# A new opening, and output and last down projections taken one token tile after the other, in a two-layer hybrid decoder trunk

## The chip, the cores and the metric

The kernel runs on one core of a Trainium2 chip. Five engines with queues of their own matter here: PE (matrix products and transposes), DVE (vector operations), ACT (scalar operations, which also copies and squares), POOL (small scalar work) and SP (issues transfers). The metric is the device time of one execution in microseconds. Times of single instructions come from one profiled execution.

## The reference

Two decoder layers run over 256 tokens of width 1024, all in float32. What is computed, cut to what matters:

```python
def hybrid_layer(x, ...):
    h = rms_norm(x, attn_pre_gain)
    u = h @ w_in                       # q, k, v of two mixers, gates: 4120 columns
    o_a = swa_sink_attention(...)      # sliding window, with sinks
    o_b = nsa_attention(...)           # compressed + selected + window branches
    mixed = sigmoid(g_a) * (o_a @ w_branch_a) + sigmoid(g_b) * (o_b @ w_branch_b)
    x = x + rms_norm(mixed @ w_out, attn_post_gain)
    h = rms_norm(x, ffn_pre_gain)
    x = x + rms_norm(conv_ffn(h, ffn_w_up, ffn_conv_w, ffn_conv_b, ffn_w_down), ffn_post_gain)
    return x

def rms_norm(x, gain):
    return x * rsqrt(mean(x * x) + EPS) * gain
```

## The kernel before, in words

The 256 tokens are two tiles, t=0 and t=1, of 128. A float32 product is done as three faster products: each operand is split into a rounded high part and the rest, the low part, and `mm3` adds high x high, high x low and low x high. Every weight therefore passes through three steps: a transfer into one of four raw buffers (`st`), a copy on ACT that makes the high part (L114), and a subtraction on DVE that makes the low part (L117). `Stream` keeps the weights in their order of use; `make` does the two splitting steps, and `W.load` the transfer. Most weights go to rings of four high and four low buffers (`wh`, `wl`); a tag in the stream sends a few elsewhere: `kB` (one buffer), `sg` (two buffers, which also hold the gates SG during attention), `q8`. A buffer of a ring can be written again once the last reader of what it held is done.

A layer runs in this order: nine input tiles (`in_tile`, chunks c=0 to 3 of the weights for both token tiles), attention units placed by a table of ticks among them, the two branch products, the output projection (`out_layer`, eight chunks k of `w_out`, for both token tiles, into PSUM banks O for t=0 and S for t=1), the norm after it, the norm before the feed-forward part, and `ffn_layer` (22 column pairs j up, convolution, gate, down).

The order in the source gives only a priority. A scheduler writes the order of each engine's instructions ahead of time, from its own idea of when operands and buffers are there; each engine then executes its list strictly in order. Only the first input tile (L866) is written out by hand for PE, DVE and ACT: there the list follows the source.

At the seam between attention and feed-forward each token tile passes a chain (`after`, L943): two squares of the product on ACT (L362), the reciprocal root on POOL (L354, L355), the residual on DVE (L397), two squares of the new x, the root again, the scaling of x by gain and root (L950, L957), eight transposes on PE (L373), high copy on ACT and low subtraction on DVE (L114, L117). Only then can the first up products (`up_first`) of that tile start.

At the beginning `start` runs zero products to warm TensorE (`warm`), transposes x (`first_T`, L410), scales it by the gain (L412) and splits it (`first_split`); `hooks` places the further pieces between the products of the first tile. `rest` computes the squares of x and the rotary tables, which end on POOL (L348, L349); the rotation of the queries (L466) waits for those.

Of the kernel before, what the change touches and what calls it, by code (L numbers as in the profile page):

```python
# [50 lines left out]
MANUAL0 = {mybir.EngineType.PE, mybir.EngineType.DVE, mybir.EngineType.Activation}  # L51
PLAN = {'A': (23, 24, 24, 34), 'B0': (39, 43), 'B1': (49, 53, 58, 64), 'C': 66, 'S': (56, 75)}
DL = {'qa0': 2, 'qa1': 13, 'ka': 6, 'qb0': 8, 'qr0': 8, 'qb1': 2, 'qr1': 4, 'cb0': 1, 'cb1': 3, 'ks': 1, 'kw': 6, 'pT': (3, 3, 2), 'pv': 4, 'hT': 1, 'ge': 3, 'pj': 4, 'cT': 5, 'cv': 9, 'yT': 1, 'h0': 5, 'h1': 4, 'uf': 0, 'x0': 3, 'x1': 3}
WARM = (6, 8)
HOOKS = {0: '1C', 1: 'B2', 2: 'D', 6: '3r'}
FIRST = [(0, 0), (0, 1), (1, 0), (1, 1), (0, 2), (1, 2), (0, 3), (1, 3)]
CMPI = (0, 0, 0, 0, 4, 6, 7, 8)
AH = (2, 2, 2, 3, 2, 2, 2, 2, 2)
TG = True
# [6 lines left out]
def tile_hybrid_trunk(  # L66
# [78 lines left out]
    class Stream:  # L145
        def __init__(self):
            self.specs, self.loaded, self.made, self.used, self.front = [], {}, {}, 0, 0

        def add(self, src, a, b, tag="w", ahead=2):
            self.specs.append((src, a, b, tag, ahead))  # L150
# [1 line left out]

        def load(self, i):
            src, a, b, tag, _ = self.specs[i]
            st = wp.tile([P, a, b], F32, tag="st", bufs=4, name=nm("st"))
            nc.sync.dma_start(st, src)
            self.loaded[i] = st, a, b, tag

        def make(self, i=None):
            i = self.front if i is None else i  # L160
# [3 lines left out]
        def high(self, i):  # L164
            if i not in self.loaded:
                self.load(i)
            st, a, b, tag = self.loaded.pop(i)
            both = None
            if tag == "w":
                hi = wp.tile([P, a, b], F32R, tag="wh", name=nm("wh"))  # L170
                lo = wp.tile([P, a, b], F32R, tag="wl", name=nm("wl"))
            elif tag in ("q8", "kB"):
                both = ap_.tile([P, 2, a, b], F32R, tag=tag, bufs=TAGS[tag], name=nm(tag))
                hi, lo = both[:, 0], both[:, 1]
            elif tag == "joint":
# [12 lines left out]
            return low
# [11 lines left out]
    def stream_layer(l):  # L200
        off = 0
        jn = 0

        def joint(at_):
            nonlocal jn
            while jn < 8 and CMPI[jn] <= at_:
                W.add(cmp_w1[l, jn].rearrange("p (i h) -> p i h", i=4), 4, P, "joint")
                jn += 1

        for i, (c0, w) in enumerate(IN_TILES):  # L210
            for c in range(4):
                if i == 6:
                    joint(2 * c)
                W.add(w_in[l, off:off + 2 * P * w].rearrange("(p k n) -> p k n", p=P, k=2), 2, w,
                      ahead=0 if i == 1 and c < 2 or i == 0 and l == 0 else AH[i])
                off += 2 * P * w
            if i == 6:
                joint(8)
        for wb in (w_branch_a, w_branch_b):
            v = wb[l].rearrange("(k p) n -> p k n", p=P)  # L220
            for n in range(2):
                for c in range(2):
                    W.add(v[:, 2 * c:2 * c + 2, n * 512:(n + 1) * 512], 2, 512)
        wo = w_out[l].rearrange("(k p) n -> p k n", p=P)
        for k in range(8):
            W.add(wo[:, k:k + 1, :], 1, D, {2: "kB", 5: "sg"}.get(k, "w"), ahead=1 if k > 5 else 2)
        wd = ffn_w_down[l].rearrange("(j p) n -> p j n", p=P)
        wu = ffn_w_up[l]
        for c in range(4):
            W.add(wu[c].rearrange("p (k n) -> p k n", k=2), 2, 512, "q8" if c == 0 else "w", ahead=0)  # L230
        for j in range(2, NJ):
            for half in range(2):
                W.add(wu[2 * j + half].rearrange("p (k n) -> p k n", k=8), 8, P, ahead=0 if j < 3 else 2)
            if LAG <= j < NJ - 2:
                W.add(wd[:, j - LAG:j - LAG + 1, :], 1, D)
        for j in range(NJ - 4, NJ):
            early[l, j] = W.add(wd[:, j:j + 1, :], 1, D, {NJ - 1: "sg", NJ - 2: "kB"}.get(j, "w"))
# [19 lines left out]
    pool.memset(rows, 0.0)  # L257
    grow = k1()[0:KD, 0:P]
    nc.sync.dma_start(cst[:, 0:P], consts[:, 0:P])
    act.dma_start(halves(X[:, 0, :])[0], halves(xv[:, 0, :])[0])  # L260
    nc.sync.dma_start(grow, attn_pre_gain[0].rearrange("(k p) -> k p", p=P))
    W.load(0)
    nc.sync.dma_start(halves(X[:, 0, :])[1], halves(xv[:, 0, :])[1])
    W.load(1)
    nc.sync.dma_start(X[:, 1, :], xv[:, 1, :])
    W.load(2)
    W.load(3)
    last_sq = [None]

    def table(fn):  # L270
# [150 lines left out]
    def attn_layer(l, xp, rs, gains, first):  # L421
# [2 lines left out]
        SG = [ap_.tile([P, QKV], F32, tag="sg", bufs=2, name=nm("SG")) for _ in range(2)]  # L424
        done = set()

        def in_tile(i, tag, fin, tmajor=False, hooks={}):
            c0, w = IN_TILES[i]
            bk = [bank(tag) for _ in range(2)]
# [2 lines left out]
            def go(t, c):  # L432
                if c not in chs:
                    chs[c] = W.next(2, w)
                ch = chs[c]
                tk = slice(t * P, (t + 1) * P)
                for k in range(2):
                    kk = 2 * c + k
                    o, wh, wl = bk[t][:, :w], ch[0][:, k, :], ch[1][:, k, :]
                    if i == 2:  # L440

                        o = o.rearrange("p (y x d) -> p y x d", x=2, y=2)
                        wh, wl = [v.rearrange("p (x y d) -> p y x d", x=2, y=2) for v in (wh, wl)]
                    mm3(o, xh[:, kk, tk], xl[:, kk, tk], wh, wl, kk == 0, kk == 7)
                if c == 3:
                    fin(t, bk[t])
                if tmajor and t == 1 and c < 2:
                    W.make()
# [477 lines left out]
    def out_layer(l, yp, gains):  # L926
# [16 lines left out]
        def after(t):  # L943
            gf = gains["ffn_pre"]
            post_norm(t, res[t], gains["attn_post"])
            xg = k4()
            s2 = mean_sq(halves(X[:, t, :]))
            for n in range(2):
                c = slice(n * 512, (n + 1) * 512)
                dve.tensor_tensor(xg[:, c], X[:, t, c], gf[:, c], ALU.mult)  # L950
            if TG and t == 1:
                with tc.issue_after(last_sq[0].ins):
                    table(AF.Gelu_apprx_tanh)
            r = rstd_of(s2)
            for n in range(2):
                c = slice(n * 512, (n + 1) * 512)
                dve.tensor_scalar(xg[:, c], xg[:, c], r, None, ALU.mult)  # L957
            later(DL["h0"] if t == 0 else DL["h1"], lambda: t8(xg, hp, t))

        order = [(0, k) for k in range(6)] + [(1, 0), (1, 1), (0, 6), (1, 2), (0, 7), (1, 3), (1, 4), (1, 5), (1, 6), (1, 7)]  # L960
        for t, k in order:
            part(lambda: go(t, k))
            if (t, k) in ((0, 7), (1, 4), (1, 5), (1, 7)):
                W.make()
        return hp


    def ffn_layer(l, hp, gains, last):
# [94 lines left out]
        for j in range(2, NJ):  # L1063
# [6 lines left out]
            if j < NJ - 2:  # L1070
                for t in range(2):
                    part(lambda: down(j - LAG, t))
        order = [(NJ - 4, 0), (NJ - 3, 0), (NJ - 2, 0), (NJ - 4, 1), (NJ - 1, 0), (NJ - 3, 1), (NJ - 2, 1), (NJ - 1, 1)]
        rs = [None, None]
        order_ = [None]
        xp = None if last else (big8("x8", 2), big8("x8", 2))
# [40 lines left out]
    def start():  # L1117
# [9 lines left out]
        gb = bank("T")  # L1127
        pe.transpose(gb[:, 0:KD], grow, ident[0:KD, 0:KD])
        dve.tensor_copy(gfirst, gb[:, 0:KD])
        low = first_split(0, 0, first_T(0, 0), xp)  # L1130
        warm(WARM[1])
        lw = W.high(0)
        low()
        lw()

        def xs(*args):
            lows = [first_split(t, h, first_T(t, h), xp) for t, h in args]
            for f in lows:
                f()

        def rest():
            for t in range(2):
                rs[t] = rstd_of(mean_sq(halves(X[:, t, :])))
            dve.tensor_scalar(nsink, sink, -1.0, None, ALU.mult)
            rope_tables()
        act_ = {"B": lambda: xs((0, 1)), "C": lambda: xs((1, 0)), "D": lambda: xs((1, 1)), "X": lambda: xs((1, 0), (1, 1)),
                "1": lambda: W.make(1), "2": lambda: W.make(2), "3": lambda: W.make(3), "r": rest, "w": lambda: warm(3)}
        return {FIRST[i]: [act_[c] for c in h] for i, h in HOOKS.items()}

    more_rows()  # L1150
    later(20, lambda: load_vec(0, 4))
# [84 lines left out]
```

## Time and profile before

| | |
|---|---|
| median of three runs | 794.11 us (791.46 to 797.75) |
| profiled execution, its own time | 794.85 us |
| its span, first to last instruction | 793.0 us |
| PE busy | 765.7 us, 97% of the span |
| DVE busy / ACT busy | 613.2 us / 495.4 us |
| mean granted TensorE clock | 0.992 of full |

The span is a little shorter than the time, since it leaves out what lies before the first and after the last instruction. A busy PE is not PE at its peak: its clock has two levels, and the granted clock of a stretch says which it is.

### The profile page before, as it was taken

How to read it: one execution, taken by the hardware profiler on the slowest of the kernel's cores; microseconds unless marked ns; L12 is line 12 of the kernel's file. 1: busy time of each engine (PE TensorE's matmuls, PEld its weight loads, DVE VectorE, ACT ScalarE, POOL GpSimd, SP SyncE). 2: the span in 40 equal slices, each digit the busy share in tenths (PEclk: the TensorE clock that was granted, in tenths of full speed). 3: DMA queues.
4: the chain of work that ended last, by engine and by line, in shares of the span. 5: the costliest groups of instructions: out<-in, count | busy, mean ns of one | idle time of the engine just before them, and what ended most of it. 6: DMA issues, size and time to landing. Idle time of an engine off the chain costs nothing.

```text
span 793.0 us, 12908 instructions
## 1 busy us (share of the span) xinstructions
PE 765.7 (97%) x4745; PEld 682.0 (86%) x4745; DVE 613.2 (77%) x1168; ACT 495.4 (62%) x948; POOL 48.1 (6%) x96
## 2 busy tenths in 40 slices
PE   8999999999899999999989999999998999999996
PEld 6689888888699999999868889888877999999995
DVE  5898888676778767777788888886867877778775
ACT  4678877744666555665555879767555655556552
POOL 2300022100100000000010000230001000000000
PEclk9999999999999999999999999999999999999999
DMA  7633156456556656666435232644645666656731
GB/s 268 218 111 123 41 160 216 144 172 205 166 168 196 187 185 183 209 218 186 157 118 173 74 121 86 206 151 135 205 137 182 193 185 186 186 184 212 216 105 53
DMA packets 42202, 131.26 MB, mean 166 GB/s; under 512 B 5359, under 2 KB 5915, under 8 KB 42139
## 3 DMA queue, kind: packets, MB, share of 16 engines
q1 hardware_dynamic: 41995, 130.18, 51.4%
q8 instruction: 37, 0.61, 0.3%
q10 hardware_dynamic: 144, 0.26, 0.1%
q14 instruction: 26, 0.21, 0.1%
HBM read 129.37 MB, written 1.05 MB: 164 GB/s over the span
## 4 chain that ended last, share of the span: by engine, by line
PE 81%; DVE 7%; ACT 7%; POOL 2%; issue 2%; DMA 1%; SPq 0%; DVEq 0%; POOLq 0%; ACTq 0%
PE mm L366 6%; PE mm L367 6%; PE mm L368 6%; PE S L367 5%; PE S L368 5%; PE S L366 5%; PE T L1000 5%; PE T L999 5%; PE mm L1000 5%; PE mm L999 5%; PE T L998 5%; PE mm L998 5%; PE O L366 3%; PE O L367 3%; PE O L368 3%; DVE wl L117 2%
## 5 line engine op out<-in xcount | busy, mean ns | idle before, releaser
L117 DVE TENSOR_TENSOR wl<-st,wh 128x1024 fp32r<-128x1024 f32 (+2 forms) x226 | 268.0, 1188 | 101.1 <-ACT wh L114 99.7
L114 ACT ACTIVATE wh<-st 128x1024 fp32r<-128x1024 f32 (+2 forms) x226 | 231.8, 1029 | 170.9 <-PE O L368 40.1
L366 PE MATMUL mm<-wh,x 128*128 128x512 f32 (+2 forms) x256 | 97.3, 382 | 0.1
L367 PE MATMUL mm<-wl,x 128*128 128x512 f32 (+2 forms) x256 | 96.2, 376 | 0.0
L368 PE MATMUL mm<-wh,x 128*128 128x512 f32 (+2 forms) x256 | 95.2, 372 | 0.0
L999 PE MATMUL mm<-q,wh 128*128 128x256 f32 x320 | 90.7, 283 | 0.0
L999 PE MATMUL T<-q,wh 128*128 128x256 f32 x320 | 90.6, 283 | 0.0
L1000 PE MATMUL T<-q,wl 128*128 128x256 f32 x320 | 90.6, 283 | 0.0
L1000 PE MATMUL mm<-q,wl 128*128 128x256 f32 x320 | 90.5, 283 | 0.0
L998 PE MATMUL T<-q,wh 128*128 128x256 f32 x320 | 90.5, 283 | 0.0
L998 PE MATMUL mm<-q,wh 128*128 128x256 f32 x320 | 90.4, 283 | 0.0
L998 PEld LDWEIGHTS mm<-q,wh 128*128 128x128 f32 x320 | 61.3, 192 | 0.9
L998 PEld LDWEIGHTS T<-q,wh 128*128 128x128 f32 x320 | 61.4, 192 | 0.8
L999 PEld LDWEIGHTS mm<-q,wh 128*128 128x128 f32 x320 | 61.3, 192 | 0.8
L999 PEld LDWEIGHTS T<-q,wh 128*128 128x128 f32 x320 | 61.4, 192 | 0.7
L1000 PEld LDWEIGHTS mm<-q,wl 128*128 128x128 f32 x320 | 61.3, 192 | 0.1
L1000 PEld LDWEIGHTS T<-q,wl 128*128 128x128 f32 x320 | 61.4, 192 | 0.0
L368 PEld LDWEIGHTS mm<-wh,x 128*128 128x128 f32 x256 | 49.2, 192 | 6.3
L366 PEld LDWEIGHTS mm<-wh,x 128*128 128x128 f32 x256 | 49.2, 193 | 5.8 <-ACT k L114 0.4
L367 PEld LDWEIGHTS mm<-wl,x 128*128 128x128 f32 x256 | 49.4, 193 | 5.6 <-DVE wl L117 0.3
L607 ACT ACTIVATE k<-k,mn 128x128 f32<-128x128 f32 (+1 forms) x96 | 42.5, 446 | 8.4 <-DVE mn L604 8.4
L354 POOL TENSOR_SCALAR rstd<-s 128x1 f32<-128x1 f32 x16 | 6.1, 381 | 520.7 <-ACT k L362 520.5
(293 smaller groups left out, 1672.9 us busy)
## 6 DMA issues: line engine op xcount, KB each, us to landing
st<-in_ffn_w_up_dram SPq DMA_DIRECT2D x88, 512.0 KB, 4.3
st<-in_w_in_dram SPq DMA_DIRECT2D x48, 512.0 KB, 3.8
st<-in_ffn_w_down_dram SPq DMA_DIRECT2D x44, 512.0 KB, 4.3
st<-in_w_out_dram SPq DMA_DIRECT2D x16, 512.0 KB, 3.6
st<-in_w_in_dram SPq DMA_DIRECT2D x16, 384.0 KB, 3.1
st<-in_cmp_w_dram SPq DMA_DIRECT2D x16, 256.0 KB, 2.6
st<-in_w_branch_a_dram SPq DMA_DIRECT2D x8, 512.0 KB, 3.6
st<-in_w_branch_b_dram SPq DMA_DIRECT2D x8, 512.0 KB, 3.6
```

Of the source, the lines that this page charges most:

```text
L114: act.activation(dst, src, AF.Copy, scale=scale)
L117: dve.tensor_tensor(dst, a, b, ALU.subtract)
L354: pool.tensor_scalar(r, s2[:, 0:1], s2[:, 1:2], EPS, ALU.add, ALU.add)
L366: pe.matmul(o, xh, wh, start=first, stop=False, skip_group_check=True)
L367: pe.matmul(o, xh, wl, start=False, stop=False, skip_group_check=True)
L368: pe.matmul(o, xl, wh, start=False, stop=last, skip_group_check=True)
L607: last_exp[0] = act.activation(self.pt[:, hh, s, :], sm[:, :nk], AF.Exp, bias=self.mn[:, i:i + 1], scale=-1.0, accum_out=self.dn[:, i:i + 1])
L998: pe.matmul(o, wh[:, k, :], hh[:, k, c0:c1], start=(k == 0), stop=False, skip_group_check=True)
L999: pe.matmul(o, wh[:, k, :], hl[:, k, c0:c1], start=False, stop=False, skip_group_check=True)
L1000: pe.matmul(o, wl[:, k, :], hh[:, k, c0:c1], start=False, stop=(k == 7), skip_group_check=True)
```

## The change

What it does, part by part:

- The order of the first loads and of the first products is new. All four halves of x are issued by ACT, in the order half 0 of both tiles, then half 1; SP issues the four weight chunks. Six more chunks (4 to 9) are loaded early, straight into the buffers of `sg` and `kB`, which attention uses later. Fewer warming products run (6, 2 and 3 instead of 6 and 8), the products of chunk 0 for both token tiles are mixed in the order in which their operands come up, and the rotary tables are asked for one step earlier.
- In `out_layer` the order is t=0 with all eight chunks, then t=1 with all eight. Chunk 6 goes to `sg`, as chunk 5 does, and chunk 7 is split between the buffers `kA` and `vbd`.
- The last four down products go t=0 first, then t=1.
- The second norm scales x by root and gain in one operation of two tensors, instead of a product with the gain before the root is known and a product with the root after it.

```diff
-WARM = (6, 8)
-HOOKS = {0: '1C', 1: 'B2', 2: 'D', 6: '3r'}
-FIRST = [(0, 0), (0, 1), (1, 0), (1, 1), (0, 2), (1, 2), (0, 3), (1, 3)]
+WARM = (6, 2, 3)
+FIRST = [(0, 0), (1, 0), (0, 1), (1, 1), (0, 2), (1, 2), (0, 3), (1, 3)]
+EARLY = {4: ("sg", 2), 6: ("sg", 2), 8: ("kB", 1)}
...
+        def early(self, i, tag, bufs):
+            both = ap_.tile([P, 2, 2, 512], F32, tag=tag, bufs=bufs, name=nm("early"))
+            self.room[i], self.room[i + 1] = both[:, 0], both[:, 1]
...
+            elif tag == "split":
+                hi = ap_.tile([P, a, b], F32R, tag="kA", name=nm("kA"))
+                lo = ap_.tile([P, a, b], F32R, tag="vbd", name=nm("vbd"))
...
-            W.add(wo[:, k:k + 1, :], 1, D, {2: "kB", 5: "sg"}.get(k, "w"), ahead=1 if k > 5 else 2)
+            W.add(wo[:, k:k + 1, :], 1, D, {2: "kB", 5: "sg", 6: "sg", 7: "split"}.get(k, "w"))
...
-    act.dma_start(halves(X[:, 0, :])[0], halves(xv[:, 0, :])[0])
     nc.sync.dma_start(grow, attn_pre_gain[0].rearrange("(k p) -> k p", p=P))
-    W.load(0)
-    nc.sync.dma_start(halves(X[:, 0, :])[1], halves(xv[:, 0, :])[1])
-    W.load(1)
-    nc.sync.dma_start(X[:, 1, :], xv[:, 1, :])
-    W.load(2)
-    W.load(3)
+    for h in range(2):
+        for t in range(2):
+            act.dma_start(halves(X[:, t, :])[h], halves(xv[:, t, :])[h])
+    for i in range(4):
+        W.load(i)
...
+    for i, (tag, bufs) in EARLY.items():
+        W.early(i, tag, bufs)
+        W.load(i)
+        W.load(i + 1)
...
+        def products(t, c, bk, chs, w):
+            todo = [(tt, p, k) for p in ((0, 0), (0, 1), (1, 0)) for tt in range(2) for k in range(2)] if c == 0 else \
+                   [(t, p, k) for p in ((0, 0), (1, 0), (0, 1)) for k in range(2)]
...
-            for n in range(2):
-                c = slice(n * 512, (n + 1) * 512)
-                dve.tensor_tensor(xg[:, c], X[:, t, c], gf[:, c], ALU.mult)
...
             r = rstd_of(s2)
             for n in range(2):
                 c = slice(n * 512, (n + 1) * 512)
-                dve.tensor_scalar(xg[:, c], xg[:, c], r, None, ALU.mult)
+                dve.scalar_tensor_tensor(xg[:, c], X[:, t, c], r, gf[:, c], ALU.mult, ALU.mult)
...
-        order = [(0, k) for k in range(6)] + [(1, 0), (1, 1), (0, 6), (1, 2), (0, 7), (1, 3), (1, 4), (1, 5), (1, 6), (1, 7)]
-        for t, k in order:
-            part(lambda: go(t, k))
-            if (t, k) in ((0, 7), (1, 4), (1, 5), (1, 7)):
-                W.make()
+        for t in range(2):
+            for k in range(8):
+                part(lambda: go(t, k))
+                if t == 1 and k in (0, 2, 5, 7):
+                    W.make()
...
-        order = [(NJ - 4, 0), (NJ - 3, 0), (NJ - 2, 0), (NJ - 4, 1), (NJ - 1, 0), (NJ - 3, 1), (NJ - 2, 1), (NJ - 1, 1)]
+        order = [(j, t) for t in range(2) for j in range(NJ - 4, NJ)]
...
-        low = first_split(0, 0, first_T(0, 0), xp)
+        m0 = first_T(0, 0)
+        lw0 = W.high(0)
+        low0 = first_split(0, 0, m0, xp)
         warm(WARM[1])
-        lw = W.high(0)
-        low()
-        lw()
+        low1 = first_split(1, 0, first_T(1, 0), xp)
+        warm(WARM[2])
+        lw0()
+        low0()
+        low1()
+        W.make(1)
...
+        steps = {2: [second], 4: [lambda: W.make(3)], 5: [rest]}
```

The scheduler turns this into the lists that the engines execute. Three places of them follow. In names such as `sg_2272` the last number counts the buffers of the program.

PE, output projection of layer 1, before: t=0 (banks O) ends with chunk 7 (`wh_2307`); t=1 (banks S) then still has chunks 3 to 7 to do.

```order
L366 MATMUL O_2222<-wh_2307,x_523_2007 128x512
L367 MATMUL O_2222<-wl_2308,x_523_2007 128x512
L368 MATMUL O_2222<-wh_2307,x_524_2008 128x512
L366 MATMUL O_2223<-wh_2307,x_523_2007 128x512
L367 MATMUL O_2223<-wl_2308,x_523_2007 128x512
L368 MATMUL O_2223<-wh_2307,x_524_2008 128x512
L366 MATMUL S_2224<-wh_2241,x_523_2007 128x512
```

The same place with the change; `sg_2260` and `sg_2261` are the high and low part of chunk 5, `sg_2272` and `sg_2273` those of chunk 6.

```order
L379 MATMUL S_2220<-sg_2260,x_520_2002 128x512
L380 MATMUL S_2220<-sg_2261,x_520_2002 128x512
L381 MATMUL S_2220<-sg_2260,x_521_2003 128x512
L379 MATMUL O_2217<-sg_2272,x_520_2002 128x512
L379 MATMUL O_2218<-sg_2272,x_520_2002 128x512
L379 MATMUL S_2219<-sg_2272,x_520_2002 128x512
L379 MATMUL S_2220<-sg_2272,x_520_2002 128x512
L380 MATMUL O_2217<-sg_2273,x_520_2002 128x512
```

In the source t=0 goes through all its chunks first. In the list the chunks 0 to 5 of both tiles come first, and the first product of chunk 6, for t=0 too, stands behind the last product of t=1 with chunk 5. The same stands in layer 2.

PE, the end of the output projection with the change: the last product of t=0 (`O_2218`), then what is left of t=1, then the transposes of t=0.

```order
L381 MATMUL O_2218<-kA_2284,x_521_2003 128x512
L380 MATMUL S_2219<-sg_2273,x_520_2002 128x512
L381 MATMUL S_2219<-sg_2272,x_521_2003 128x512
L380 MATMUL S_2220<-sg_2273,x_520_2002 128x512
L381 MATMUL S_2220<-sg_2272,x_521_2003 128x512
L379 MATMUL S_2219<-kA_2284,x_520_2002 128x512
L380 MATMUL S_2219<-vbd_2285,x_520_2002 128x512
L381 MATMUL S_2219<-kA_2284,x_521_2003 128x512
L379 MATMUL S_2220<-kA_2284,x_520_2002 128x512
L380 MATMUL S_2220<-vbd_2285,x_520_2002 128x512
L381 MATMUL S_2220<-kA_2284,x_521_2003 128x512
L386 MATMUL T_2364<-cst,k_592_2319 128x128 x4
```

Ten products stand between the last of t=0 and its transposes; before there were 24, and another six behind the transposes.

ACT, the same place with the change: the high parts of the first up weights (`q_598`, `wh_2354` to `wh_2499`), chunk 6 of the output weights (`sg_2272`), the squares of t=0.

```order
L114 ACTIVATE q_598_2337<-st_2335 128x1024
L114 ACTIVATE wh_2354<-st_2352 128x1024
L114 ACTIVATE wh_2392<-st_2390 128x1024
L114 ACTIVATE wh_2435<-st_2433 128x1024
L114 ACTIVATE wh_2499<-st_2497 128x1024
L114 ACTIVATE sg_2272<-st_2270 128x1024
L375 ACTIVATE k_588_2307,s_587_2306<-O_2217 128x512
```

Before, `wh_2373` stood between the squares of the product and those of x, and two more up weights behind those. Chunk 6 now stands behind five up weights in ACT's list.

DVE, end of the first input tile, before: `wl_322` is the low part of chunk 4, `wl_346` and `wl_352` of 5 and 6; L466 is the rotation that needs the table from POOL.

```order
L342 TENSOR_SCALAR k_89_253<-k_89_253 128x64
L117 TENSOR_TENSOR wl_322<-st_319,wh_321 128x1024
L466 SCALAR_TENSOR_TENSOR k_90_280<-mm_159,rstd_240,tab 128x512
L468 SCALAR_TENSOR_TENSOR k_91_281<-mm_159,rstd_240,tab 128x8x32 x2
L117 TENSOR_TENSOR wl_346<-st_343,wh_345 128x1024
```

With the change (`wl_327` to `wl_357` are chunks 4 to 7):

```order
L117 TENSOR_TENSOR wl_327<-early_98,wh_326 128x1024
L353 TENSOR_SCALAR k_92_254<-k_92_254 128x64
L117 TENSOR_TENSOR wl_349<-early_98,wh_348 128x1024
L354 SCALAR_TENSOR_TENSOR k_92_254<-k_92_254 128x64
L117 TENSOR_TENSOR wl_353<-early_101,wh_352 128x1024
L355 TENSOR_SCALAR k_92_254<-k_92_254 128x64
L117 TENSOR_TENSOR wl_357<-early_101,wh_356 128x1024
L493 SCALAR_TENSOR_TENSOR k_93_287<-mm_179,rstd_241,tab 128x512
```

All four chunks of the second input tile now stand ahead of the rotation (L493 is the old L466); before only one did.

## Rows read from the trace of the kernel before

**Rows 1.** Page, part 1: busy us, share, instructions.
```profile
PE 765.7 (97%) x4745; PEld 682.0 (86%) x4745; DVE 613.2 (77%) x1168; ACT 495.4 (62%) x948; POOL 48.1 (6%) x96
```
**Rows 2.** What PE waited for: us in total, times, longest us.
```profile
PE mm L368 <- DVE q L117: 2.8, 2, 1.4
...
PE S L367 <- DVE wl L117: 1.9, 2, 1.4
PE T L373 <- DVE k L957: 1.9, 4, 0.5
...
PE mm L366 <- ACT q L114: 0.5, 2, 0.3
```
**Rows 3.** Timeline, seam of layer 1: start us, us, engine, line; idle before in brackets.
```profile
196.91 0.39 PE L368 MATMUL O<-wh,x 128*128 128x512 f32 x1
...
202.34 0.39 PE L368 MATMUL S<-wh,x 128*128 128x512 f32 x1
...
203.22 1.06 PE L373 MATMUL T<-cst,k 128*128 128x128 f32 x8 [0.48 <-DVE k L957]
203.38 3.49 DVE L117 TENSOR_TENSOR wl<-st,wh 128x1024 fp32r<-128x1024 f32 x3
...
205.28 0.40 PE L368 MATMUL S<-wh,x 128*128 128x512 f32 x1
...
207.53 0.50 PE L368 MATMUL mm<-q,q 128*128 128x512 f32 x1 [1.39 <-DVE q L117]
...
213.25 1.07 PE L373 MATMUL T<-cst,k 128*128 128x128 f32 x8 [0.45 <-DVE k L957]
```
**Rows 4.** Timeline, the seam: the first ring buffer that chunk 0 gave back.
```profile
191.67 1.06 ACT L114 ACTIVATE wh<-st 128x1024 fp32r<-128x1024 f32 x1 [0.62 <-PE S L368]
```
**Rows 5.** Durations by line: ns min/median/max, and the page's transfers: us to landing.
```profile
L114 ACT ACTIVATE wh<-st x226: 663/1060/1087, 7.5 to 769.8; 128x1024 fp32r<-128x1024 f32 x101, 128x768 fp32r<-128x768 f32 x8, 128x560 fp32r<-128x560 f32 x4
...
L117 DVE TENSOR_TENSOR wl<-st,wh x226: 732/1225/1229, 8.5 to 770.9; 128x1024 fp32r<-128x1024 f32 x101, 128x768 fp32r<-128x768 f32 x8, 128x560 fp32r<-128x560 f32 x4
...
L957 DVE TENSOR_SCALAR k<-k,rstd x8: 480/484/489, 202.6 to 602.1; 128x512 f32<-128x512 f32 x8
...
L397 DVE SCALAR_TENSOR_TENSOR X<-k,rstd,X x16: 743/747/753, 199.1 to 789.3; 128x512 f32<-128x512 f32 x16
...
st<-in_ffn_w_up_dram SPq DMA_DIRECT2D x88, 512.0 KB, 4.3
```
**Rows 6.** Stretches: us, PE busy (matmuls), granted clock, DMA share, GB/s.
```profile
56.86:60.27 3.41, 3.41 (x18) 0.50 0.00 0
401.60:405.02 3.42, 3.42 (x11) 0.50 0.46 152
...
206.00:208.00 2.00, 0.61 (x3) 1.00 0.79 246
```
**Rows 7.** Timeline of PE at the seam between the layers.
```profile
399.49 0.66 PE L373 MATMUL T<-cst,k 128*128 128x128 f32 x4 [1.58 <-DVE k L405]
...
401.42 0.99 PE L373 MATMUL T<-cst,k 128*128 128x128 f32 x4 [1.27 <-DVE k L405]
```
**Rows 8.** Timeline of PE, the beginning.
```profile
5.06 1.11 PE L410 MATMUL T<-cst,X 128*128 128x128 f32 x4
...
5.83 3.58 PE L1124 MATMUL S<-k 128*128 128x512 f32 x8
...
11.16 0.48 PE L366 MATMUL mm<-wh,x 128*128 128x512 f32 x1
...
23.09 0.39 PE L368 MATMUL mm<-wh,x 128*128 128x512 f32 x1
```
**Rows 9.** Timeline of DVE and PE, second input tile.
```profile
26.15 0.75 DVE L466 SCALAR_TENSOR_TENSOR k<-mm,rstd,tab 128x512 f32<-128x512 f32 x1 [1.82 <-POOL tab L348]
...
28.88 0.50 PE L367 MATMUL S<-wl,x 128*128 128x512 f32 x1 [1.44 <-DVE wl L117]
```
**Rows 10.** Timeline of PE, first attention units of layer 1.
```profile
56.34 0.53 PE L477 MATMUL T<-ident_r,k 128*128 128x128 f32 x4 [1.08 <-ACT q L114]
```

More of the change, by code (lines that the diff above doesn't have):

```diff
@@ L154, in load @@
             src, a, b, tag, _ = self.specs[i]
-            st = wp.tile([P, a, b], F32, tag="st", bufs=4, name=nm("st"))
+            st = self.room.pop(i, None)
+            if st is None:
+                st = wp.tile([P, a, b], F32, tag="st", bufs=4, name=nm("st"))
             nc.sync.dma_start(st, src)
             self.loaded[i] = st, a, b, tag
+        def early(self, i, tag, bufs):
+            both = ap_.tile([P, 2, 2, 512], F32, tag=tag, bufs=bufs, name=nm("early"))
+            self.room[i], self.room[i + 1] = both[:, 0], both[:, 1]
         def make(self, i=None):
@@ L425, in attn_layer @@
         done = set()
+        def products(t, c, bk, chs, w):
+            todo = [(tt, p, k) for p in ((0, 0), (0, 1), (1, 0)) for tt in range(2) for k in range(2)] if c == 0 else \
+                   [(t, p, k) for p in ((0, 0), (1, 0), (0, 1)) for k in range(2)]
+            if c == 0:
+                todo = todo[6 * t:6 * t + 6]
+            for tt, (xp_, wp_), k in todo:
+                tk = slice(tt * P, (tt + 1) * P)
+                pe.matmul(bk[tt][:, :w], (xh, xl)[xp_][:, 2 * c + k, tk], chs[c][wp_][:, k, :],
+                          start=(c == k == xp_ == wp_ == 0), stop=False, skip_group_check=True)
         def in_tile(i, tag, fin, tmajor=False, hooks={}):
@@ L436, in go @@
                 tk = slice(t * P, (t + 1) * P)
+                if first and i == 0 and c < 2:
+                    products(t, c, bk, chs, w)
+                    return
                 for k in range(2):
@@ L1129, in start, with second @@
         dve.tensor_copy(gfirst, gb[:, 0:KD])
-        low = first_split(0, 0, first_T(0, 0), xp)
+        m0 = first_T(0, 0)
+        lw0 = W.high(0)
+        low0 = first_split(0, 0, m0, xp)
         warm(WARM[1])
-        lw = W.high(0)
-        low()
-        lw()
-        def xs(*args):
-            lows = [first_split(t, h, first_T(t, h), xp) for t, h in args]
+        low1 = first_split(1, 0, first_T(1, 0), xp)
[4 more added lines that the diff above has]
+        W.make(1)
+        def second():
+            m0, m1 = first_T(0, 1), first_T(1, 1)
+            lw = W.high(2)
+            lows = [first_split(t, 1, m, xp) for t, m in ((0, m0), (1, m1))]
+            lw()
             for f in lows:
@@ L1145, in rest @@
             rope_tables()
-        act_ = {"B": lambda: xs((0, 1)), "C": lambda: xs((1, 0)), "D": lambda: xs((1, 1)), "X": lambda: xs((1, 0), (1, 1)),
-                "1": lambda: W.make(1), "2": lambda: W.make(2), "3": lambda: W.make(3), "r": rest, "w": lambda: warm(3)}
-        return {FIRST[i]: [act_[c] for c in h] for i, h in HOOKS.items()}
+        steps = {2: [second], 4: [lambda: W.make(3)], 5: [rest]}
+        return {FIRST[i]: fns for i, fns in steps.items()}
     more_rows()
```

1 line of the change is left out of this document (added).

## The prediction

> **What bounds the kernel.** First the page's first part: PE is busy 97% of the span [rows 1], so no other engine can be the bound, and a change is worth what it adds to or takes from the times in which PE stands still or runs at half clock. DVE and ACT matter only where PE waits for them. Second, the waits of PE and its timeline: the places that this change touches are the opening, the second input tile and the seam between attention and feed-forward, once per layer. The waits for "q" and "k" belong to the seam, half of them in either layer; the two for "wl" (1.9) are both in the second input tile of layer 1 [rows 2]. Third, the timeline of one seam [rows 3], and the granted clock of three stretches [rows 6].
>
> One unit comes from there: 24 products lie between the last of t=0 at 196.91 and the last before the transposes at 202.34 [rows 3], so a product takes 5.43/24 = 0.23 us, although each row says 0.39: they overlap.
>
> **The seam, per layer.** This is where the change loses. It says that t=0 takes all eight chunks first; the emitted list says otherwise. Chunk 6 goes to `sg`, whose two buffers hold chunk 5, and those are free only when t=1 is through chunk 5 too. So the list is t=0 and t=1 with chunks 0 to 5, then chunk 6 for both, then the rest. Four costs follow.
>
> 1. *Waiting for chunk 6.* Before (1,5) ends, 72 products now run where 66 ran up to the last of t=0, which was at 196.91; so it ends at about 196.91 + 6 x 0.23 = 198.3, and PE then has nothing but chunk 6. Its high copy stands on ACT behind five up weights. One of the four raw buffers is held by chunk 6 itself, so the load of the fifth up weight can only be issued when the first of the five has been split. That is when chunk 0's ring buffer is back: 191.67 [rows 4] + 1.06 + 1.23 [rows 5] = 194.0, and landing 4.3 us later, at 198.3. ACT copies it (to 199.4), then chunk 6 (to 200.4), DVE subtracts (to 201.7). PE has four high products to do meanwhile, so it could have started the low ones at about 198.3 + 5 x 0.23 = 199.4: **2.4 us** of waiting (1.3 if the load comes early and the copy starts when the buffer is free, 2.8 if DVE is taken).
> 2. *The chain of t=0 uncovered.* From the last product of t=0 to its transposes 6.31 us passed (196.91 to 203.22), with only 0.48 of waiting since 24 products lay there [rows 3]. Now ten lie there. The chain is longer by the difference of the one-operation scaling to the old one, first half: the nearest row is L397, also two tensors and a scalar, at 0.747, against 0.484 for L957 [rows 5]: +0.26. If the new operation were as fast as the old, +0. So 6.31 + 0.26 − 0.23 (the product itself) − 10 x 0.23 = **4.05 us** (3.8 to 4.5, the ends being a scaling as fast as the old one and one that is 0.7 longer).
> 3. *The split behind the transposes.* Six products stood between the transposes and the first up product, and PE still waited 1.39 [rows 3]. Now none do; but the cause of the 1.39 was in part the three low parts (3.49 us) that DVE did first. Without those, one copy and one subtraction of half a width remain, and the second half of the scaling comes 0.75 behind the first: **0.6** (0.4 to 1.5, the upper end being the old wait with its cover gone).
> 4. *The transposes of t=1.* Its chain took 7.97 us (205.28 to 213.25 [rows 3]). Now it starts 2.3 us behind that of t=0, and every square and residual of it queues on ACT and DVE behind t=0's. PE has only t=0's up products as cover. **1.0** (0.3 to 2.0), an estimate between the present 0.45 and a chain longer by one full set of t=0's steps.
>
> Sum 8.05. What falls away are the present waits of the seam: q 2.8, k 1.9, q 0.5 for both layers [rows 2], so (2.8 + 1.9 + 0.5)/2 = **2.6** per layer. Net **+5.5 per layer** (3.2 to 8.2, the sums of the ends), **+11.0 for both**; all ends of a kind at once are unlikely, and I use two thirds of the way to them, 7.9 to 14.6.
>
> What the change takes off DVE here, two gain products of x, costs nothing before either: they ran beside ACT's squares. I count 0.
>
> **The opening.** PE runs transposes (5.06, 1.11 us), eight warming products (3.58, so 0.45 each) and the first product at 11.16; the first tile ends with a product at 23.09 [rows 8]. Now PE's own list in front of the first product is transposes, two warming products, transposes, three: 5.06 + 1.11 + 0.9 + 1.11 + 1.35 = 9.5, if the operands are there by then. With 48 products of 0.23 and eight transposes of about 1.06, the tile ends at about 21.4 instead of 23.3: **−1.9** (0 if the weights of chunk 0 are late, since x now shares the first transfers). In the second tile PE waited 1.44 for a low part, because DVE first sat 1.82 in front of the rotation, waiting for POOL's table [rows 9]. With the change four low parts stand ahead of that rotation: both waits for low parts (1.9 [rows 2]) go, **−1.9** (−1.0 if another chunk is late). Sum **−3.8** (−2 to −4.5).
>
> **The first attention units.** PE waits 1.08 at 56.34 [rows 10], and 3.41 us at half clock follow [rows 6], worth half of it, 1.7. With PE some 4 us earlier and nothing else shifted the wait could stay, shrink or grow. The list there is unchanged. **−1.0** (−3.0 to 0).
>
> **Costed at nothing.** The last down products with t=0 first: in layer 1 the emitted PE list at that end is what it was; in layer 2 four products change places, and the chain behind the last product is the same. If that cover is wrong, t=0's chain would end one product earlier or later, 0.2 us.
>
> **Sum.** 11.0 − 3.8 − 1.0 = +6.2 on the profiled execution's 794.85 gives 801.05. That execution is 0.74 above the median of 794.11, so the forecast is **800.3 us**.
>
> **A rule that speaks against it.** The clock stayed at 1.00 in the seam at 206 to 208 although PE was busy only 0.61 of 2 us, behind waits of 0.48 and 1.39; it fell to 0.50 for 3.42 us at 401.60, behind waits of 1.58 and 1.27 [rows 3, 6, 7]. The new seam has waits of 2.4 and 4.05, both beyond the second case, so a fall is likely in both layers, 2 x 1.7 = 3.4 us, unless PE then waits for t=1 anyway, when it is free; the 1.0 of step 4 has about half of it. The Trainium skill, "TensorE: Matmul & The Clock Gate", Part 1, says that half rate is the default and that sustained activity releases it. By that rule the seams would pay the 3.4 in full, the trace at 401.60 agrees, and the one at 206 does not contradict it.
>
> **Rivals.**
> A. *The opening pays for the seams.* If chunk 6 waits 1.3, the scaling is no longer than before and t=1's chain hides, a seam costs 1.3 + 3.8 + 0.6 + 0.3 − 2.6 = 3.4, both 7; the opening gives 3.8 to 4.5 and the attention wait with its slow stretch goes, 3. Net about 0: **794**, not slower. For it: the half-clock stretch follows one short wait only. Against: DVE's and ACT's lists behind the transposes. Chance 0.20.
> B. *Half clock in both seams, not hidden.* Place: the up products of t=0 behind the 4.05 us wait. It decides if t=1's transposes are ready before PE gets there: +3.4, and with the late load at its upper end: **804** to 806. For it the stretch at 401.60; against it the one at 206. Chance 0.22.
> C. *The change does what it says:* t=0's chunks all come first, its chain lies under 48 products of t=1, 11 us, more than 6.31. Then all 2.6 of waiting per layer goes, less 0.7 for the split: −3.8, with the opening −4.8: about **785.5**. Against it is the emitted list itself. Chance 0.05.
> The forecast keeps 0.53.
>
> **Numbers.** Of this kernel a difference under about 1%, 7.9 us, can't be told from no change. A lies within; the forecast's own spread (7.9 to 14.6 less 2 to 7.5) crosses +7.9 in about three of ten; B crosses it in most: slower 0.53 x 0.32 + 0.22 x 0.9 = 0.37; faster 0.05; within 1% 0.58. The range leaves out C and the ends of A and B: **793.5 to 806.5**.
>
> **What would show it.** In each output projection a PE wait for `sg` (ACT, then DVE) of about 2.4, before the last product of t=0; a wait of about 4 us of the norm's transposes for DVE's new scaling; the first product near 9.5 and the first tile done near 21.4; no wait for a low part in the second tile; the half-clock stretch at 56.9 there or gone, and new ones at the seams or not. I am wrong if PE shows no wait at chunk 6, or if products other than these ten are found between t=0's last and its transposes.

## The result: 801.39 us, 0.9% above the kernel before

| | before | after |
|---|---|---|
| median | 794.11 us (five runs beside those of the change, 791.46 to 797.75) | 801.39 us (five, 800.33 to 802.39) |
| span of the profiled execution | 793.0 us | 799.6 us |
| PE busy | 765.7 us | 767.8 us |
| granted TensorE clock, mean | 0.992 | 0.988 |

The ratio is 1.0088, with a 95% interval of 1.0065 to 1.0112. Measured again later (`e10_after`) it was 1.0097 (1.0073 to 1.0121).

The page's first part, to be set against [rows 1], and the longest waits of PE (us in total, times, longest), against [rows 2]:

```profile
PE 767.8 (96%) x4742; PEld 682.8 (85%) x4742; DVE 610.5 (76%) x1160; ACT 495.3 (62%) x948; POOL 51.3 (6%) x96
```

```profile
PE T L386 <- DVE k L981: 7.6, 3, 3.7
PE O L379 <- ACT sg L114: 4.7, 2, 2.5
...
PE O L380 <- DVE sg L117: 0.5, 2, 0.3
```

PE is still the bound. The old waits of the seam (q) and of the second tile (wl) are gone; 7.6 + 4.7 + 0.5 us stand in their place, all in the two seams.

A table by stage tells where the time went. Its boundaries are points that every kernel passes: PE's wait of about 1.7 us for the compression (its product with `wj` starts at 116.17 and 505.13 before, 110.26 and 505.90 after), PE's wait of about 1.6 us after layer 1 (399.49 [rows 7], 400.31), and the end of the span. The stage with a layer's seam also holds its feed-forward part; the third holds the seam between the layers and layer 2's attention.

| stage, us | before | after | difference |
|---|---|---|---|
| opening and attention, layer 1 | 116.17 | 110.26 | −5.91 |
| seam and feed-forward, layer 1 | 283.32 | 290.05 | +6.73 |
| attention, layer 2 | 105.64 | 105.59 | −0.05 |
| seam and feed-forward, layer 2 | 287.87 | 293.70 | +5.83 |
| span | 793.0 | 799.6 | +6.6 |

These are single executions. The trace of `e10_after`, the same kernel, has its seam stages +6.97 and +6.69 longer than before instead of +6.73 and +5.83, so such a difference is known to about one microsecond.

**The opening.** Timeline of PE and DVE after (start us, us, engine, line; idle before in brackets), against [rows 8, 9]:

```profile
4.62 1.11 PE L423 MATMUL T<-cst,X 128*128 128x128 f32 x4
...
5.38 1.14 PE L1148 MATMUL S<-k 128*128 128x512 f32 x2
...
6.36 0.60 PE L423 MATMUL T<-cst,X 128*128 128x128 f32 x4
6.71 0.94 PE L1148 MATMUL S<-k 128*128 128x512 f32 x3
...
7.88 1.26 PE L448 MATMUL mm<-wh,x 128*128 128x512 f32 x4 [0.22 <-ACT x L114]
...
19.67 0.39 PE L381 MATMUL mm<-wh,x 128*128 128x512 f32 x1
```

```profile
24.54 0.75 DVE L493 SCALAR_TENSOR_TENSOR k<-mm,rstd,tab 128x512 f32<-128x512 f32 x1 [1.59 <-POOL tab L361]
...
29.43 0.51 PE L504 MATMUL T<-ident_r,k 128*128 128x128 f32 x4 [0.99 <-DVE k L117]
```

The first product runs at 7.88 instead of 11.16 and the first tile ends 3.4 us earlier. In the second tile the wait for low parts has become one of 0.99 for the rotated queries (the first input tile holds queries), which still wait for POOL's table.

**The seam.** Timeline of layer 1 after, against [rows 3, 4]:

```profile
192.10 0.39 PE L381 MATMUL S<-sg,x 128*128 128x512 f32 x1
...
192.94 1.06 ACT L114 ACTIVATE wh<-st 128x1024 fp32r<-128x1024 f32 x1 [1.62 <-DMA st<-in_ffn_w_up_dram]
193.90 1.04 ACT L114 ACTIVATE sg<-st 128x1024 fp32r<-128x1024 f32 x1
...
194.99 0.73 PE L379 MATMUL O<-sg,x 128*128 128x512 f32 x2 [2.50 <-ACT sg L114]
...
196.44 0.51 PE L380 MATMUL O<-sg,x 128*128 128x512 f32 x1 [0.25 <-DVE sg L117]
...
198.65 0.39 PE L381 MATMUL O<-kA,x 128*128 128x512 f32 x1
...
200.94 0.39 PE L381 MATMUL S<-kA,x 128*128 128x512 f32 x1
...
204.11 1.42 DVE L981 SCALAR_TENSOR_TENSOR k<-X,rstd,gain 128x512 f32<-128x512 f32 x2 [1.83 <-POOL rstd L368]
...
205.01 1.94 PE L386 MATMUL T<-cst,k 128*128 128x128 f32 x8 [3.68 <-DVE k L981]
...
206.78 0.80 PE L379 MATMUL mm<-q,q 128*128 128x512 f32 x1
...
213.94 1.04 PE L386 MATMUL T<-cst,k 128*128 128x128 f32 x8
```

To be seen, from the top: t=1 is through chunk 5 at 192.10; ACT sits 1.62 for the load of an up weight, copies that first, and only then chunk 6; PE stands 2.50 for the high part and 0.25 for the low one. Then t=0's last product (198.65), ten products, and 3.68 of waiting. The transposes take 1.94 instead of 1.06. Granted clock of the stretches there and in layer 2's seam (PE busy, PEld, DVE, ACT, POOL, clock, DMA share, GB/s):

```profile
204.00:206.00 2.00, 0.99 (x5) 1.02 (x6) 1.89 (x3) 0.19 (x2) 1.65 (x3) 0.57 0.00 0
206.00:208.00 2.00, 2.00 (x8) 1.53 (x7) 1.20 (x3) 1.20 (x2) 0.00 (x0) 0.50 0.04 8
208.00:210.00 2.00, 2.00 (x7) 1.52 (x6) 2.00 (x4) 0.34 (x1) 0.00 (x0) 0.50 0.04 14
210.00:212.00 2.00, 2.00 (x8) 1.62 (x7) 0.23 (x1) 1.98 (x5) 0.82 (x2) 0.72 0.74 246
```

```profile
600.00:602.00 2.00, 1.53 (x8) 1.56 (x8) 1.59 (x3) 0.41 (x1) 1.32 (x2) 0.56 0.00 0
602.00:604.00 2.00, 2.00 (x7) 1.40 (x7) 1.62 (x3) 0.78 (x2) 0.00 (x0) 0.59 0.00 0
```

0.50 is the lower level, 1.2 GHz. PE fell to it in both seams, where before it did in neither. What is missing to 1.00 in these rows is 2 x (0.43 + 0.50 + 0.50 + 0.28) = 3.4 us in layer 1 and 2 x (0.44 + 0.41) = 1.7 in layer 2. PE still stood waiting when the two falls began; stretches of 0.1 us, weighted with PE's busy time, leave 3.05 and 1.59 of PE's time. Layer 2's waits are those of layer 1 but for size:

```profile
590.48 0.73 PE L379 MATMUL O<-sg,x 128*128 128x512 f32 x2 [2.20 <-ACT sg L114]
591.93 0.50 PE L380 MATMUL O<-sg,x 128*128 128x512 f32 x1 [0.25 <-DVE sg L117]
600.47 1.94 PE L386 MATMUL T<-cst,k 128*128 128x128 f32 x8 [3.67 <-DVE k L981]
608.41 1.29 PE L386 MATMUL T<-cst,k 128*128 128x128 f32 x8 [0.23 <-DVE k L981]
```

### The profile page after: what moved, and what is told of

It reads as the page before. It is cut to its first block, busy times and chain, and to the rows that moved or that the text cites. A ratio compares the mean times of both kernels' runs of the same rounds, so it can differ in the third digit from the quotient of the medians.

```text
span 799.6 us, 12893 instructions
## 1 busy us (share of the span) xinstructions
PE 767.8 (96%) x4742; PEld 682.8 (85%) x4742; DVE 610.5 (76%) x1160; ACT 495.3 (62%) x948; POOL 51.3 (6%) x96
## 4 chain that ended last, share of the span: by engine, by line
PE 78%; ACT 8%; DVE 6%; POOL 3%; DMA 2%; issue 2%; DVEq 0%; SPq 0%; POOLq 0%; ACTq 0%
PE mm L380 6%; PE mm L379 6%; PE mm L381 6%; PE T L1024 5%; PE mm L1024 5%; PE T L1023 5%; PE mm L1023 5%; PE T L1022 5%; PE mm L1022 5%; PE S L380 4%; PE S L381 4%; PE S L379 4%; PE O L380 3%; PE O L381 3%; PE O L379 3%
## 5 line engine op out<-in xcount | busy, mean ns | idle before, releaser
L117 DVE TENSOR_TENSOR wl<-st,wh 128x1024 fp32r<-128x1024 f32 (+2 forms) x216 | 256.0, 1186 | 109.6 <-ACT wh L114 108.1
L114 ACT ACTIVATE wh<-st 128x1024 fp32r<-128x1024 f32 (+2 forms) x216 | 221.7, 1028 | 180.1 <-PE mm L1023 40.1
L379 PE MATMUL mm<-wh,x 128*128 128x512 f32 (+2 forms) x248 | 93.5, 378 | 0.1
L380 PE MATMUL mm<-wl,x 128*128 128x512 f32 (+2 forms) x248 | 92.5, 373 | 0.1
L381 PE MATMUL mm<-wh,x 128*128 128x512 f32 (+2 forms) x248 | 91.8, 371 | 0.0
L381 PEld LDWEIGHTS mm<-wh,x 128*128 128x128 f32 x248 | 47.2, 190 | 5.9
L379 PEld LDWEIGHTS mm<-wh,x 128*128 128x128 f32 x248 | 47.3, 191 | 5.5 <-ACT k L114 0.4
L380 PEld LDWEIGHTS mm<-wl,x 128*128 128x128 f32 x248 | 47.4, 191 | 5.3 <-DVE wl L117 0.3
```

Of the source, the lines that this page charges most:

```text
L114: act.activation(dst, src, AF.Copy, scale=scale)
L117: dve.tensor_tensor(dst, a, b, ALU.subtract)
L379: pe.matmul(o, xh, wh, start=first, stop=False, skip_group_check=True)
L380: pe.matmul(o, xh, wl, start=False, stop=False, skip_group_check=True)
L381: pe.matmul(o, xl, wh, start=False, stop=last, skip_group_check=True)
```

## The experiments

All ratios are to the kernel before, on the same chip. "Seams" are the two seam stages of the table above, as differences to before.

**Making the change do what it says.** A buffer of `sg` holds 8 KB per partition, and a high or low part takes 4, yet each part took a buffer of its own. One word lets both parts share one (`e1_pair`), so that chunk 5 and chunk 6 fit at once (it does the same to the last down weight, which goes to `sg` too):

```diff
-            elif tag in ("q8", "kB"):
+            elif tag in ("q8", "kB", "sg"):
```

> The changed kernel with one edit: high and low part of a chunk share one sg buffer, so chunk 5 takes one and chunk 6 the other, and t=0 really goes through all eight chunks first. My theory (the seam's loss comes from chunk 6 being locked out of sg until t=1 is through chunk 5): both waits for sg (2.75 and 2.45) and nearly all of the two waits of 3.7 before the transposes go, the seams become about 2 us shorter than before the change, and with the opening's 5.9 the time is about 9.7 below the kernel before, near 784.5. Rival 1 (t=0 first costs as much by itself, since loads and splits for the up weights come late): no better than the opening alone, 788 or more. Rival 2 (the loss is the one-operation scaling and the clock): still 798 or more.

Measured: 785.91 us, ratio 0.9898 (0.9880 to 0.9917). Seams −1.04 and −1.13. Timeline of PE in layer 1's seam, from the last product of t=0 on:

```profile
187.15 0.39 PE L381 MATMUL O<-kA,x 128*128 128x512 f32 x1
...
193.66 1.29 PE L386 MATMUL T<-cst,k 128*128 128x128 f32 x8 [0.68 <-DVE k L981]
...
206.35 1.29 PE L386 MATMUL T<-cst,k 128*128 128x128 f32 x8 [1.18 <-DVE k L981]
```

PE's list now has all of t=0's chunks first. No wait for `sg` is left, and 0.68 of the 3.68. So t=0 first was not the loss; that it did not come first was. This one word is worth some 15 us against the change as made (0.9898 against 1.0088). The gain per seam is 1.1, not the 2 expected: besides the 0.68, t=1's transposes now wait 1.18, where before they waited 0.45.

**The parts apart.** `e2_start` has the changed opening and the old rest; `e3_seam` the reverse.

> The changed opening alone; output projection, norm and last down products as before. My theory: the trace puts the opening and the first attention units 5.9 us ahead, nothing later depends on it, so 5.9 below the kernel before, near 788. Rival (the gain is taken back by waits later in the layer, or is one of a single profiled run): within 2 us of before.

Measured: 789.70, ratio 0.9949 (0.9932 to 0.9965); by the trace its first stage takes 110.48 and its span 787.6, so −5.7 and −5.4.

> The kernel before with the changed output projection, norm and last down products, and its old opening. My theory: the two seams cost 6.7 and 5.8, independent of the opening: 12.5 above the kernel before, near 806.5. Rival (the seam loses only because the opening's early loads or shifted phase of the clock act on it): 801 or less.

Measured: 808.92, ratio 1.0189 (1.0167 to 1.0211); seams +7.28 and +7.44, span 804.6, +11.6. The two spans add up to the whole (−5.4 + 11.6 = +6.2, against +6.6), but in part by luck: in the trace of `e3_seam` layer 2's attention stage is 2.4 shorter than before, without the two clock falls that the last section tells of. The times did not quite add up: −4.0 and +15 against +7.0. So the changed kernel and `e3_seam` ran once more, on one chip.

> The changed kernel again, on one chip with the next one. If the parts add up, it stands 5.7 below the next one (the opening by the trace), and 6 to 7.5 above the kernel before. If the time of e3_seam was real and the opening is worth more where the seams are bad, 7.5 or more below the next one.

> The kernel of e3_seam again. If the parts add up: 12 to 13 above the kernel before. If e3's time stands: 15 above.

Measured: 801.70, ratio 1.0097 (1.0073 to 1.0121), and 806.37, ratio 1.0154 (1.0127 to 1.0182). So the seam part is +12.2 here, and with −4.0 the whole would be +8.2, where +7.7 was measured: the parts add up within their intervals. `e10_after` stands 4.7 below `e11_seam`, not 5.7 and not 7.5. The first +15 (13.2 to 16.7) and the +12.2 (10.1 to 14.5) overlap; in the traces `e3_seam` lost 14.7 in its seams and `e11_seam` 12.6. The opening is worth 4 to 5.7 us; the runs don't tell it closer.

**The price of the clock.** `e4_seamwarm` keeps PE busy with sixteen products that nobody reads:

```diff
+        zb = bank("mm")
+        for _ in range(16):
+            pe.matmul(zb, yp[0][:, 0, 0:P], yp[0][:, 0:2, :].rearrange("p a b -> p (a b)"), start=True, stop=True, skip_group_check=True)
         return hp
```

> The changed kernel with 16 products whose result nobody reads, written to a free bank, between the last product of t=1 and the transposes of t=0 in either layer, where PE stood still 3.7 us; they run beside the wait. Both theories: no fall to half clock behind it. My theory (the slow stretch is nearly hidden, since the transposes of t=1 are not ready much earlier): 1.2 us are gained in layer 1, none in layer 2, and new waits for t=1's transposes of 1 to 2 us appear; about 1.2 below the changed kernel. Rival B (half clock is paid in full): 4 to 5 below the changed kernel, no new waits.

Measured: 798.18, ratio 1.0053 (1.0034 to 1.0073); seams +5.03 and +4.94. The scheduler put seven of the sixteen into the wait for chunk 6 and nine behind t=1. Timeline and clock of layer 1's seam:

```profile
205.11 1.30 PE L386 MATMUL T<-cst,k 128*128 128x128 f32 x8 [1.64 <-DVE k L981]
...
212.41 1.29 PE L386 MATMUL T<-cst,k 128*128 128x128 f32 x8 [0.39 <-DVE k L981]
```

```profile
202.00:206.00 4.00, 2.32 (x13) 1.56 (x12) 2.17 (x4) 2.52 (x9) 2.38 (x4) 1.00 0.01 2
```

The clock stays at 1.00; t=0's transposes start where they did (205.11, 205.01), those of t=1 1.5 us earlier. So half clock cost 290.05 − 288.35 = 1.7 us in layer 1 and 293.70 − 292.81 = 0.9 in layer 2, a little over half of the 3.05 and 1.59 that it took from PE. `e10_after` says the same of other falls: its seams lost 3.27 and 2.91 of PE's time to half clock, and its stages (290.29 and 294.56) are 1.9 and 1.75 longer than those of `e4_seamwarm`. The rest was hidden, in layer 1 in part because t=1's transposes would not have been ready much sooner: at full clock they wait 0.39 and take 1.29 instead of 1.04. The remainder of it stands in no row. I had expected 1.2 and 0, rival B the whole; it lies between.

**The load ahead of chunk 6.** `e5_fewmake` asks for four up weights behind all of t=1's products, not among them:

```diff
-                if t == 1 and k in (0, 2, 5, 7):
-                    W.make()
+        for k in range(4):
+            W.make()
```

> The changed kernel with the four early splits of up weights asked for behind all the products of t=1; in ACT's list chunk 6 then stands behind three up weights that are ready early, not behind the one whose load is late. My theory (the wait for sg is longer than its own copy because of that load): the wait for sg falls from 2.75 to about 1.6 in layer 1 and from 2.45 to about 1.6 in layer 2. The first up weight is split late instead, behind the transposes of t=0, and may cost 1 to 2 us there. Rival (the wait is the copy and subtraction of chunk 6 alone): still 2.4 to 2.8.

Measured: 807.08, ratio 1.0163 (1.0145 to 1.0182). Timeline of PE in its seam of layer 1:

```profile
194.14 0.74 PE L379 MATMUL O<-sg,x 128*128 128x512 f32 x2 [1.32 <-ACT sg L114]
195.59 0.51 PE L380 MATMUL O<-sg,x 128*128 128x512 f32 x1 [0.24 <-DVE sg L117]
204.15 1.75 PE L386 MATMUL T<-cst,k 128*128 128x128 f32 x8 [3.68 <-DVE k L981]
206.41 0.80 PE L379 MATMUL mm<-q,q 128*128 128x512 f32 x1 [0.50 <-ACT q L114]
209.84 0.79 PE L380 MATMUL mm<-q,q 128*128 128x512 f32 x1 [2.64 <-DVE q L117]
```

The wait for chunk 6 falls from 2.75 to 1.56, as said (in layer 2 from 2.45 to 1.80): the late load was 1.2 us of it in layer 1 and 0.65 in layer 2. The first up weight's split then costs 0.50 + 2.64 (0.78 + 2.64 in layer 2), more than the 1 to 2 expected, and the kernel gets slower.

**The scaling in one operation.** `e6_oldnorm` is the changed kernel with the two-operation scaling of before (the diff ahead, undone at that place).

> The changed kernel with the second norm scaled in two operations as before. My theory (the one-operation scaling stands on the chain, 0.71 against 0.44 for each half, and parts the eight transposes, 1.29 against 1.07): the wait before the transposes of t=0 falls from 3.7 to 3.4 and those transposes close up, 0.4 to 0.5 us per layer, about 1 below the changed kernel, too little to tell by the times. Rival (the two gain products cost DVE as much, ahead of the residual of t=1): no less than the changed kernel, and the wait 3.7 or more.

Measured: 802.12, ratio 1.0090 (1.0071 to 1.0109). The wait before the transposes is 3.94 in both layers, not 3.4, as the rival said, but for another reason. Timeline of layer 1:

```profile
202.08 0.58 ACT L375 ACTIVATE k<-S 128x512 f32<-128x512 f32 x1
...
202.65 0.62 ACT L375 ACTIVATE k<-X 128x512 f32<-128x512 f32 x1
...
203.46 0.30 POOL L367 TENSOR_SCALAR rstd<-s 128x1 f32<-128x1 f32 x1 [2.83 <-ACT k L375]
...
205.07 1.94 PE L386 MATMUL T<-cst,k 128*128 128x128 f32 x8 [3.94 <-DVE k L984]
```

ACT's list here has a square of t=1's product (S) between the two squares of t=0's x, so POOL starts the root 0.52 later (it waits 2.83, against 2.31 with the change); the shorter scaling gives back 0.27. In layer 2 the rows are the same. So this run does not compare the two scalings alone; the next two kernels do.

**Towards a better kernel.** Both have the shared buffer and put t=0's transposes six products later; `e8_pair_on_h6` has the two-operation scaling besides:

```diff
-DL = {... 'h0': 5, ...}
+DL = {... 'h0': 6, ...}
```

> The shared sg buffer (t=0 really first), and the transposes of t=0 placed six products later. My theory: the wait of 0.68 in front of them falls to zero, since six products are 1.4 us, and nothing else waits for them: 1.3 us below the kernel with the shared buffer alone. Rival (the first up products then wait for the split of t=0): nothing gained, and a new wait of about 0.7 in front of them.

> As the one before, and the second norm scaled in two operations as before the change. My theory: the wait of t=1's transposes falls from 1.18 to 0.9 and they close up by 0.2, so 2 x 0.5 below the one before, about 2.3 below the kernel with the shared buffer alone, near 783.5: the best of all. Rival (DVE's two more operations per tile delay what stands behind them): the same as the one before or above.

Measured: 785.00, ratio 0.9879 (0.9864 to 0.9893), and 784.69, ratio 0.9868 (0.9850 to 0.9886). The six products take away the wait of 0.68, and the seams get 1.2 and 0.9 shorter than those of `e1_pair` in the trace, too little for the times. The two scalings are alike, so the 0.5 per layer expected of the second kernel did not come: t=1's transposes wait 1.35 there instead of 0.9. Timeline of layer 1's t=1, one operation (`e7_pair_h6`):

```profile
202.93 0.30 POOL L367 TENSOR_SCALAR rstd<-s 128x1 f32<-128x1 f32 x1 [2.31 <-ACT k L375]
...
203.89 1.42 DVE L981 SCALAR_TENSOR_TENSOR k<-X,rstd,gain 128x512 f32<-128x512 f32 x2 [1.83 <-POOL rstd L368]
...
204.79 1.29 PE L386 MATMUL T<-cst,k 128*128 128x128 f32 x8 [1.18 <-DVE k L981]
```

and two (`e8_pair_on_h6`):

```profile
201.93 1.28 DVE L977 TENSOR_TENSOR k<-X,gain 128x512 f32<-128x512 f32 x2
...
202.87 0.50 POOL L367 TENSOR_SCALAR rstd<-s 128x1 f32<-128x1 f32 x1 [2.31 <-ACT k L375]
...
204.04 0.88 DVE L984 TENSOR_SCALAR k<-k,rstd 128x512 f32<-128x512 f32 x2 [0.83 <-POOL rstd L368]
...
204.67 1.06 PE L386 MATMUL T<-cst,k 128*128 128x128 f32 x8 [1.35 <-DVE k L984]
```

With two operations the gain product is on DVE when POOL starts the root, and POOL's first step takes 0.50 instead of 0.30. That eats most of what the shorter scaling gives; wait and transposes together are 2.47 and 2.41.

**The early loads.** `e9_noearly` is `e2_start` without the six:

```diff
-EARLY = {4: ("sg", 2), 6: ("sg", 2), 8: ("kB", 1)}
+EARLY = {}
```

> The changed opening alone (as e2_start), without the six early loads into sg and kB: chunks 4 to 9 go through the four raw buffers as before. DVE's list then has one low part ahead of the first rotation, as before the change, not four. My theory (the early loads remove the second tile's waits, the new order of the first tile gives the rest): first product at about 8 as with the loads; waits for low parts of some 2 us in the second tile come back, so the opening and attention units gain 3.5 to 4 against before, not 5.7. Rival (the waits go because the tables are asked for earlier): no wait for a low part, 5.7 as with the loads.

Measured: 789.94, ratio 0.9941 (0.9922 to 0.9959), no different from `e2_start`. The wait for a low part is back, but as one of 1.22. Timeline of DVE and PE:

```profile
21.69 0.75 DVE L493 SCALAR_TENSOR_TENSOR k<-mm,rstd,tab 128x512 f32<-128x512 f32 x1 [1.63 <-POOL tab L361]
...
24.41 0.50 PE L380 MATMUL S<-wl,x 128*128 128x512 f32 x1 [1.22 <-DVE wl L117]
```

The 0.99 for the rotated queries is gone. The rotation waits for POOL's table as before (1.63 and 1.59), but starts at 21.69 instead of 24.54, since the table is ready earlier: with the early loads DVE's own steps for it stand among the four low parts, and POOL's are slowed beside these (its second root step at 17.95 took 1.64 us, here 0.57). New waits of PE of 0.80 and 0.66 stand at 48.81 and 53.14. The first stage takes 110.86 instead of 110.48. So the early loads mostly trade one wait for others, and the opening's gain is that of the rest of the new opening; how much of it is the order of loads and products, the fewer warming products or the earlier tables no run tells apart. Both theories fall: the wait returned, the gain stayed.

## Why the prediction held, step by step

The forecast was 800.3 in a range of 793.5 to 806.5, as the sum of a gain of 4.8 and a loss of 11.0. By the traces the gain was 5.9 and the loss 12.6 (13.7 in `e10_after`), on the same mechanism. Both were sized low, by 1.1 and 1.6, and these misses cancel in part: that the forecast came within 1.1 us is partly luck.

- *Waiting for chunk 6:* 2.4 said, 2.75 and 2.45 measured. (The times written there, 201.7 and 199.4, give 2.3, as five products are counted where four are named; with four it is 2.5.) `e5_fewmake` shows that the late load is part of it, and `e1_pair` that the locked buffer is all of it.
- *The chain uncovered:* 4.05 said, 3.68 and 3.67 measured. From t=0's last product to its transposes 6.36 passed, against 6.31 before; the longer scaling (+0.27) was paid back by POOL (−0.2). Here the step "I count 0" for the removed gain products was wrong: they ran beside ACT's squares, as said, but also beside POOL's root. Rows of before (first two) and after:

```profile
200.46 1.28 DVE L950 TENSOR_TENSOR k<-X,gain 128x512 f32<-128x512 f32 x2
...
201.40 0.51 POOL L354 TENSOR_SCALAR rstd<-s 128x1 f32<-128x1 f32 x1 [2.31 <-ACT k L362]
...
203.14 0.30 POOL L367 TENSOR_SCALAR rstd<-s 128x1 f32<-128x1 f32 x1 [2.31 <-ACT k L375]
```

- *The split behind the transposes:* 0.6 said. No wait stands there; the late second half shows instead inside the transposes, 1.30 for 1.06 at full clock (`e4_seamwarm`), so 0.23, and as much again for those of t=1.
- *The transposes of t=1 and the clock:* 1.0 said. At full clock they wait 0.39 and 0.44 (`e4_seamwarm`), and the clock cost another 1.7 and 0.9. The fall that the part on the rule called likely came in both seams, and nearly half of its price was hidden in both. This is the term that was sized furthest too low.
- These terms (chunk 6, the chain, twice 0.23, t=1's wait at full clock and the clock) less the old 2.6 make 6.4 and 5.3; the stages lost 6.73 and 5.83. The rest, 0.3 and 0.5, I can't put to a row.
- *The opening:* first product at 9.5 said, 7.88 measured. The transposes began 0.44 earlier; I took the second transposes and the last warming products at the slow durations of [rows 8], and they ran at 0.60 and 0.31 each; and I added rows that overlap. The first tile gave 3.4 instead of 1.9. The second tile gave 1.7 (its end at 32.38 instead of 37.52, and 3.4 of that from the first): 1.9 said, but through a new wait of 0.99 that I didn't foresee. The next two tiles gave back 0.9 (50.44 against 54.72). Together 4.2, where 3.8 was said.
- *The first attention units:* 1.0 said; that tile takes 13.95 instead of 15.69, 1.7, as both the 1.08 wait and the half-clock stretch are gone.
- *Costed at nothing:* the wait between the layers, 1.57 and 1.27, is the old one, with the changed order of the last down products and (in `e2_start`) with the old.

Rival A fell because the seams cost 12.6, not 7. Rival B was right on the place, half clock in both seams, and too high on the time: half clock cost 2.6 us in one execution and 3.7 in the other, of which step 4 of the forecast already held a part, and 801.4 was measured, not 804. Rival C's price of 785.5 is near what the kernel gives when C is true, 785.9, but not by C's terms: the seams gave 2.2 instead of 3.8, and the first stage 5.5 instead of 4.8.

## What to carry to other kernels

Read a change in the emitted order, not in the source: a buffer that is free too late turns "this first" into "this last". Where one tensor tile is taken to the end to cover its chain, count the products that are left behind it; under the length of the chain, each missing product is paid in full (14 fewer here, 3.2 us at 0.23 each, and the wait rose from 0.48 to 3.68). And before a buffer is called taken, look at how much of it is used.

## What the runs showed of the hardware

- POOL's first root step takes 0.30 us with DVE idle and 0.50 beside a DVE product of two SBUF tensors (rows of `e7_pair_h6` and `e8_pair_on_h6`). The Trainium skill, "GPSIMD Engine Reference", section 8 (Key points), says that this engine shares its SBUF interfaces with VectorE and that they contend when a DVE instruction has two SBUF inputs; the trace agrees, and the price here is 0.2 us. In all runs together this step took 0.29 to 0.32 us beside no DVE instruction or beside a product of a PSUM bank and an SBUF tensor, 0.50 to 0.52 beside the product of two SBUF tensors, and 0.73 to 0.74 beside the scaling in one operation.
- The clock falls of one and the same stretch differ between executions: layer 2's attention stage, whose code is the same in all, took 105.6 us before with stretches at 0.50 around 402 and 446, 104.3 in `e10_after` with one around 446, and 103.1 in `e1_pair` with none. Such a difference, 2.5 us, is as large as a step of this prediction.
- The eight transposes of t=0 took 1.94 us at a granted clock of 0.50 (after) and 1.30 at 1.00 (`e4_seamwarm`), with the same scaling ahead of them: transposes, too, are slower at the lower clock.
